# The delta rule of the second block in chunks of 128 tokens instead of 64

## The chip, the cores and the metric

The kernel runs on one core of a Trainium2 chip, as one program that computes two transformer-like blocks after one another. The metric is the device time of one execution in microseconds (us). TensorE (PE) multiplies matrices, VectorE (DVE) and ScalarE (ACT) work elementwise, GpSimd (POOL) does a few masks and fills, and SyncE (SP) issues the transfers between HBM and the on-chip memory SBUF. PSUM holds the results of TensorE.

## What is computed

The change touches one part of the second block, the gated delta rule, for 512 tokens and 8 heads of width 128. For each head a state `S` (128x128) goes from chunk to chunk of tokens. Within a chunk, a unit lower triangular matrix must be inverted. Cut to what matters, the reference is:

```python
GDN_CHUNK = 64
g = jnp.cumsum(chunk(g), axis=-1)                     # log decay, summed inside a chunk
decay = where(causal, exp(g_i - g_j), 0)
L = where(strict, (k_beta @ k.T) * decay, 0)          # chunk x chunk
t_inv = inverse(eye + L)
u = t_inv @ v_beta
w = t_inv @ (k_beta * exp(g))
attn_intra = where(causal, (q @ k.T) * decay, 0)
q_dec = q * exp(g);  k_dec = k * exp(g_last - g)

def step(S, inp):                                     # once per chunk
    v_new = u_c - w_c @ S
    o = q_dec @ S + attn_intra @ v_new
    S = S * exp(g_last) + k_dec.T @ v_new
```

The outputs `o` don't depend on the size of the chunk except by rounding: 8 chunks of 64 tokens and 4 chunks of 128 tokens give the same function.

## The kernel before

**Around the change.** Nearly all of TensorE's work is the projection of activations by weights that come from HBM. A helper (`piece`, `mm3`, `blocks`) loads 128x1024 weights into one of five buffers `raw`, splits each into a high part (`hi`, on ScalarE, L266) and a low part (`lo`, on VectorE, L269), and multiplies by three passes: high by high (L281), high by low (L282), low by high (L284), each 128x128 by 128x512, into a PSUM bank `pp`. A piece is 24 such passes. These passes are called projection passes below. The small products of the delta rule are in full fp32: the profile has each of them as two passes (two weight loads and two matmuls), with the matrices in tiles `sc`, `tr` (PSUM), `rp`, `p`, `n` (work tiles in SBUF), `A` and `G` (big areas).

**The delta rule.** It runs in two halves of four heads (`hf` 0 and 1). For each half the tokens stand in four tiles of 128 (`T[t]`). `gdn_kk` builds minus L for each 128-token tile with masks that keep the two 64-token chunks apart (`tri`, `strict`), writes it to HBM and clears the four 32x32 blocks on the diagonal of the copy that stays (`N`). `gdn_blocks` inverts the 32x32 diagonal blocks of all chunks on VectorE, row by row (L249, L1276), and writes the result to HBM (`X_d`). `gdn_solve` (`SO(j)` for head j) loads these blocks as `XN` and, transposed, as `XT`, and adds what couples two neighbouring blocks of 32: one product `q` (L1296), a copy on ScalarE, one product `z` (L1300), one addition on VectorE (L249), then `u` (L1304) and `w` (L1307). Each of these is four matmuls, one per tile of tokens, that is eight passes.

**The steps.** `gdn_steps` goes over the chunks, four heads at a time: `wS` (L1325), `vn` on VectorE, `o` in pairs that add up in one PSUM tile (L1333 with the state, 128 rows deep; L1334 with `vn`, as deep as a chunk, 64 rows), a copy of `o` on ScalarE (L1335), `sp` (L1339, 64 rows deep) and the new state on VectorE (L1345). Between two steps the program offers one block of the gate projections (`fill`, 16 per half). After the chunks, four norms follow.

**What sets the order.** A scheduler that plays the program through when it is built sets the order of the instructions on each engine, by priority in program order and by when operands and buffers are free. On the chip each engine keeps that order, and so does each transfer queue.

`gates2` prepares the decays: sums of `g` in a chunk (by a product with `tri`), the last `g` of each chunk, and their exponentials, each by some 24 small VectorE instructions (`exp_acc`). `egl` is the exponential for the state.

Of the kernel before, what the change touches and what calls it, by code (L numbers as in the profile page):

```python
# [16 lines left out]
MUL, ADD, SUB, MAX, MIN = ALU.mult, ALU.add, ALU.subtract, ALU.max, ALU.min  # L17
# [68 lines left out]
def lay_out(inp):  # L86
    a = {k: np.asarray(v) for k, v in inp.items()}
    f = np.float32
    o = {}
    o["xT"] = a["x"][0].T.reshape(KT, 128, S)  # L90
    o["cc"] = np.stack([a["c"][0], a["c_2"][0]]).reshape(32, 128)
    o["pos"] = a["positions"].astype(np.int32)
    wada = np.concatenate([a["w_ada"], a["w_ada_2"]])

    wt = wada.transpose(0, 2, 1).reshape(3, 48, 128, 2, 1024).transpose(0, 3, 2, 1, 4)
    o["wada"] = wt.reshape(3, 2, 128, 48 * 1024)

    o["wad0"] = wt[0][:, :, :32].reshape(2, 128, 2, KT, 1024).transpose(3, 1, 2, 0, 4).reshape(KT, 128, 4096)
    inv = (10000.0 ** (-np.arange(32, dtype=f) / f(32))).astype(f)
    sign = np.repeat(np.array([-1, 1, -1, 1], f), 32)  # L100
    cols = [colvec(a["norm_g"][l]) for l in range(2)]
    cols += [colvec(a["b_ada"][l]) for l in range(2)] + [colvec(a["b_ada_2"][0])]
    cols += [colvec(a["final_g"]), colvec(a["norm_gain_2"][0])]
    cols += [colvec(a["b_glu"][l]) for l in range(2)]
    cols += [colvec(a["sub_g"][l]) for l in range(2)]
    cols += [a["conv_w_2"][0].reshape(4, 24, 128).transpose(2, 1, 0).reshape(128, 96)]
    cols += [a["gdn_norm_gain_2"][0][:, None]]
    cols += [np.concatenate([a["q_norm_gain_2"][0]] * 2)[:, None], np.concatenate([a["k_norm_gain_2"][0]] * 2)[:, None]]
    cols += [np.concatenate([inv] * 4)[:, None], sign[:, None]]
    o["vec"] = np.concatenate(cols, axis=1)  # L110
    rep = np.concatenate(
        [np.stack([a["lam_q1"], a["lam_k1"], a["lam_q2"], a["lam_k2"]], 1).reshape(-1),
         a["a_log_2"][0], a["dt_bias_2"][0], a["sinks_2"][0]])
    o["rep"] = np.broadcast_to(rep[None], (128, NREP))
    for l in range(2):
        w = a["w_in"][l]
        u, zs, q, k, v, za = np.split(w, 6, axis=1)
        o[f"wuA{l}"] = grp_blocks(u[:, :512], 512)[0]
        o[f"wuB{l}"] = grp_blocks(u[:, 512:], 512)[0]
        o[f"win{l}"] = np.concatenate([fm_blocks(t) for t in (q, k, zs, za)])  # L120
        o[f"wv{l}"] = grp_blocks(v, 512)
        o[f"wglu{l}"] = fm_blocks(a["w_glu"][l])
        wo = np.concatenate([a["w_out"][l][1024:], a["w_out"][l][:1024]])
        o[f"woA{l}"] = grp_blocks(wo[:, :512], 512)[0]
        o[f"wo{l}"] = fm_blocks(wo[:, 512:])


        def pair(t):
            return t.reshape(2, 32, 64).transpose(0, 2, 1).reshape(128, 32)
        ls = np.broadcast_to(a["ssm_log_step"][l][:, None], (64, 64))  # L130
        o[f"ssa{l}"] = np.concatenate([pair(a["ssm_a_re"][l]), pair(a["ssm_a_im"][l]), pair(ls)], axis=1)
        B = [a[n][l].reshape(2, 32, 64, 16).transpose(0, 2, 1, 3).reshape(128, 512) for n in ("ssm_b_re", "ssm_b_im")]
        C = [a[n][l].reshape(2, 32, 16, 64).transpose(0, 3, 1, 2).reshape(128, 512) for n in ("ssm_c_re", "ssm_c_im")]
        o[f"ssb{l}"] = np.concatenate(B + C, axis=1)
        o[f"ssd{l}"] = a["ssm_d"][l].T
    w2 = a["w_in_2"][0]
    sz = (1024, 1024, 1024, 1024, 8, 8, 1024, 256, 256, 1024, D, D)
    qa, ka, va, za, ba, aa, qb, kb, vb, zb, gla, glb = np.split(w2, np.cumsum(sz)[:-1], axis=1)
    o["w2t"] = grp_blocks(np.concatenate([vb, ba, aa], axis=1), 272)[0]
    o["w2"] = np.concatenate([fm_blocks(t) for t in (qa, ka, va, za, qb, kb, zb, gla, glb)])  # L140
    o["wbg"] = fm_blocks(a["w_branch_gdn_2"][0])
    o["wbs"] = fm_blocks(a["w_branch_swa_2"][0])
    o["wo2A"] = grp_blocks(a["w_out_2"][0][:, :512], 512)[0]
    o["wo2"] = fm_blocks(a["w_out_2"][0][:, 512:])
    o["relb"] = a["rel_bias_2"]
    o["onehot"] = onehot_t5()
    i, j = np.arange(128)[:, None], np.arange(128)[None]
    same = i // 64 == j // 64
    tri = (same & (i <= j)).astype(f)
    strict = (same & (j < i)).astype(f)  # L150
    sellast = (same & (i % 64 == 63)).astype(f)
    o["cst2"] = np.concatenate([tri, strict, sellast, same.astype(f)], axis=1)
    ident = np.eye(128, dtype=f)
    mask = np.zeros((128, 512), f)
    mask[:, 384:] = np.where(np.tril(np.ones((128, 128), bool)), 0.0, -1e30)
    o["cst"] = np.concatenate([ident, mask], axis=1)
    return {k: np.ascontiguousarray(v) for k, v in o.items()}
# [10 lines left out]
class Kern:  # L168
# [949 lines left out]
    def gates2(self):  # L1118
# [49 lines left out]

        ps = self.sbank("sc", 2)
        nc.tensor.matmul(ps[:, :32], self.sellast, gc, start=True, stop=True)  # L1170
        for hf in range(2):
            c = 64 * hf + 63
            nc.tensor.matmul(ps[:, 32 + 32 * hf:64 + 32 * hf], self.ident[:, c:c + 1].to_broadcast([128, 128]), gc, start=True, stop=True)
        self.bg, self.kd, self.egl = sm("bg"), sm("kd"), self.misc[:, 512:576]
        assert len(used) <= 16
        self.exp_acc(gc, sm, self.bg)
        self.tt(self.bg, self.bg, self.beta, MUL)
        self.tt(x, ps[:, :32], gc, SUB)
        self.exp_acc(x, sm, self.kd)
        nc.vector.tensor_copy(e, ps[:, 32:64])  # L1180
        self.exp_acc(e, sm, self.egl[:, 0:32])
        nc.vector.tensor_copy(e, ps[:, 64:96])
        self.exp_acc(e, sm, self.egl[:, 32:64])

    def gdn_k(self, hf, j, ps):

# [94 lines left out]
    def gdn_solve(self, hf, j):  # L1281
# [13 lines left out]
        for t in range(4):  # L1295
            nc.tensor.matmul(q[:, T[t]], N[:, T[t]], XT[:, T[t]], start=True, stop=True)  # L1296
        nc.scalar.copy(N, q)
        z = self.sbank("sc", 2)
        for t in range(4):
            nc.tensor.matmul(z[:, T[t]], XN[:, T[t]], N[:, T[t]], start=True, stop=True)  # L1300
        self.tt(XT, z, XT, ADD)
        u = self.sbank("sc", 2)
        for t in range(4):
# [7 lines left out]
    def gdn_steps(self, hf):  # L1311

        nc, G, A = self.nc, self.G, self.A
        H = [slice(j * 128, (j + 1) * 128) for j in range(4)]
        St = self.t2("n", 4)
        for c in range(8):
            t, R = c // 2, slice(64 * (c % 2), 64 * (c % 2) + 64)
            ct, cc = slice(t * 128, (t + 1) * 128), slice(c * 64, (c + 1) * 64)
            vn = self.t2("p", 4)
            u4 = G[R, 8:12, ct]  # L1320
            vn4 = vn[R].rearrange("p (j e) -> p j e", j=4)
            if c:
                wS = self.sbank("sc", 2)
                for j in range(4):
                    nc.tensor.matmul(wS[R, H[j]], G[:, j, cc], St[:, H[j]], start=True, stop=True)  # L1325
                self.stt(vn4, wS[R].rearrange("p (j e) -> p j e", j=4), -1.0, u4, MUL, ADD)
            else:
                nc.vector.tensor_copy(vn4, u4)
            o = self.sbank("tr", 2)
            for j in range(4):  # L1330
                oj = o[:, j * 64:(j + 1) * 64]
                if c:
                    nc.tensor.matmul(oj, St[:, H[j]], G[:, 4 + j, cc], start=True, stop=False)  # L1333
                nc.tensor.matmul(oj, vn[R, H[j]], G[R, 12 + j, cc], start=c == 0, stop=True)  # L1334
            nc.scalar.copy(A[:, 4 * hf:4 * hf + 4, cc], o[:, :256].rearrange("p (j c) -> p j c", j=4))  # L1335
            if c < 7:
                sp = self.sbank("tr", 2)
                for j in range(4):
                    nc.tensor.matmul(sp[:, H[j]], A[R, 12 + j, ct], vn[R, H[j]], start=True, stop=True)  # L1339
                if c == 0:  # L1340
                    nc.vector.tensor_copy(St, sp)
                else:
                    for j in range(4):
                        g = (c % 2) * 32 + t * 8 + 4 * hf + j
                        self.stt(St[:, H[j]], St[:, H[j]], self.egl[:, g:g + 1], sp[:, H[j]], MUL, ADD)  # L1345
            yield
        for j in range(4):
            oj = A[:, 4 * hf + j, :]
            r = self.rows_norm(oj, self.ones, 1.0 / 128, 1e-6, False)
            self.stt(oj, oj, self.v("gdn_g"), r, MUL, MUL)  # L1350
            yield
# [89 lines left out]
    def block2(self, acc, xs):  # L1441
# [30 lines left out]
        for hf in range(2):  # L1472
# [34 lines left out]
            SO(3)  # L1507
            fill(1)
            st = self.gdn_steps(hf)
            for j in range(12):  # L1510
                next(st, None)
                fill()
            fill(16)
# [184 lines left out]
```

## Time and profile before

| | |
|---|---|
| median of 3 runs | 3592.48 us (3590.34 to 3594.72) |
| the profiled execution | 3601.23 us, its span 3599.2 us |
| TensorE busy | 3432.1 us, 95% of the span |
| VectorE, ScalarE, GpSimd busy | 2128.8, 1185.8, 633.5 us |
| mean granted TensorE clock | 0.976 of full speed |

The span runs from the first to the last instruction of the profiled execution, and the time of that execution is 2.0 us more. A busy TensorE is not one at its peak: matmuls are pipelined, and a matmul of 128 columns and one of 64 can both be listed with some 0.28 us although the next starts much earlier. So what a product costs is read from the starts of its neighbours. The granted clock of a stretch is 1.00 at 2.4 GHz and 0.50 at 1.2 GHz; a mean between the two says how much of the stretch ran at which level.

### The profile page before, as it was taken

How to read it: one execution, taken by the hardware profiler on the slowest of the kernel's cores; microseconds unless marked ns; L12 is line 12 of the kernel's file. 1: busy time of each engine (PE TensorE's matmuls, PEld its weight loads, DVE VectorE, ACT ScalarE, POOL GpSimd, SP SyncE). 2: the span in 40 equal slices, each digit the busy share in tenths (PEclk: the TensorE clock that was granted, in tenths of full speed). 3: DMA queues.
4: the chain of work that ended last, by engine and by line, in shares of the span. 5: the costliest groups of instructions: out<-in, count | busy, mean ns of one | idle time of the engine just before them, and what ended most of it. 6: DMA issues, size and time to landing. Idle time of an engine off the chain costs nothing.

```text
span 3599.2 us, 45635 instructions
## 1 busy us (share of the span) xinstructions
PE 3432.1 (95%) x16673; PEld 2728.0 (76%) x16673; DVE 2128.8 (59%) x4157; ACT 1185.8 (33%) x2052; POOL 633.5 (18%) x885
## 2 busy tenths in 40 slices
PE   7979989999789989899999999999999999999999
PEld 4867766778679876677788887787888777788887
DVE  7994645677857436556665689724892255434432
ACT  3422323353224323333532434222532134433311
POOL 0082681002820006810002212000200000000000
PEclk9989999999899999999999999999999999999999
DMA  9858446656667855356576545322333232224442
GB/s 331 299 153 242 143 120 179 186 190 202 207 206 226 226 163 161 105 176 202 173 225 219 175 123 127 114 89 84 100 108 104 69 100 71 77 92 142 141 140 91
DMA packets 265117, 565.04 MB, mean 157 GB/s; under 512 B 76732, under 2 KB 113853, under 8 KB 264893
## 3 DMA queue, kind: packets, MB, share of 16 engines
q1 hardware_dynamic: 264894, 562.14, 50.7%
q8 instruction: 131, 2.15, 0.2%
q14 instruction: 92, 0.75, 0.1%
HBM read 497.89 MB, written 50.50 MB: 152 GB/s over the span
## 4 chain that ended last, share of the span: by engine, by line
PE 67%; DVE 11%; DMA 9%; POOL 8%; issue 3%; SPq 1%; ACT 1%; DVEq 0%; POOLq 0%; ACTq 0%
PE pp L282 18%; PE pp L281 18%; PE pp L284 18%; DMA raw<-in_wada 5%; DVE lo L269 2%; PE sc L918 1%; POOL misc L820 1%; POOL G L821 1%; POOL misc L818 1%; DVE G L249 1%; POOL misc L819 1%; DVE raw L517 1%; POOL lo L269 1%; POOL G L660 1%; PE sc L1407 1%
## 5 line engine op out<-in xcount | busy, mean ns | idle before, releaser
L281 PE MATMUL pp<-HH,hi 128*128 128x512 f32 (+1 forms) x3568 | 1395.6, 394 | 32.2 <-ACT HH L567 19.1
L282 PE MATMUL pp<-HL,hi 128*128 128x512 f32 (+1 forms) x3440 | 1339.6, 393 | 4.2 <-DVE HL L252 4.1
L266 ACT CAST hi<-raw 128x1024 fp32r<-128x1024 f32 (+1 forms) x538 | 559.7, 1043 | 1194.5 <-PE pp L282 937.5
L284 PE MATMUL pp<-HH,lo 128*128 128x512 f32 (+1 forms) x3568 | 907.8, 392 | 8.6 <-DVE lo L269 8.6
L269 DVE TENSOR_TENSOR lo<-raw,hi 128x1024 fp32r<-128x1024 f32 (+1 forms) x506 | 625.6, 1238 | 349.2 <-PE pp L284 163.9
L281 PEld LDWEIGHTS pp<-HH,hi 128*128 128x128 f32 x3568 | 678.7, 190 | 190.2 <-issue 33.2
L284 PEld LDWEIGHTS pp<-HH,lo 128*128 128x128 f32 x3568 | 659.9, 190 | 162.6 <-issue 19.8
L282 PEld LDWEIGHTS pp<-HL,hi 128*128 128x128 f32 x3440 | 654.2, 190 | 155.4 <-issue 22.1
L517 DVE CUSTOM_DVE_ANT_0 raw<-raw,cs,vec 128x1024 f32<-128x1024 f32 x112 | 158.3, 1414 | 244.0 <-DMA raw<-in_wada 238.3
L517 DVE CUSTOM_DVE_ANT_0 raw<-raw,cs,mod 128x1024 f32<-128x1024 f32 x112 | 154.6, 1381 | 248.6 <-DMA raw<-in_wada 245.3
L217 ACT ACTIVATE p<-p,st 128x128 f32<-128x128 f32 (+2 forms) x192 | 101.9, 531 | 196.9 <-DVE st L244 196.6
L1652 POOL TENSOR_TENSOR rp<-rp,n 128x512 f32<-128x512 f32 (+1 forms) x43 | 59.8, 1404 | 433.8 <-ACT n L1651 433.8
L354 PE MATMUL pp<-lo,HH 128*128 128x512 f32 (+1 forms) x320 | 121.6, 385 | 4.8 <-DVE lo L269 4.7
L353 PE MATMUL pp<-hi,HH 128*128 128x512 f32 (+1 forms) x320 | 121.1, 384 | 4.1 <-ACT HH L567 3.1
L269 POOL TENSOR_TENSOR lo<-raw,hi 128x1024 fp32r<-128x1024 f32 x32 | 77.0, 2406 | 262.8 <-PE pp L284 189.7
L355 PE MATMUL pp<-hi,HL 128*128 128x512 f32 (+1 forms) x320 | 116.3, 384 | 1.0 <-DVE HL L252 0.9
L818 POOL TENSOR_TENSOR misc<-misc,G 128x64 f32<-128x64 f32 x124 | 59.4, 479 | 313.9 <-ACT G L808 304.7
L918 PE MATMUL sc<-rp,rp 64*128 64x128 f32 (+3 forms) x256 | 92.6, 493 | 10.4 <-DVE st L920 10.4
L282 PE MATMUL pp<-A,hi 128*128 128x512 f32 x256 | 100.7, 393 | 0.0
L920 DVE CUSTOM_DVE_ANT_0 p<-sc,cst 128x128 f32<-128x128 f32 (+3 forms) x128 | 61.2, 484 | 33.7 <-PE sc L918 33.3
L354 PEld LDWEIGHTS pp<-lo,HH 128*128 128x128 f32 x320 | 62.2, 195 | 18.7 <-DVE lo L269 5.7
L353 PEld LDWEIGHTS pp<-hi,HH 128*128 128x128 f32 x320 | 61.9, 194 | 17.7 <-ACT HH L567 3.9
(325 smaller groups left out, 3944.5 us busy)
## 6 DMA issues: line engine op xcount, KB each, us to landing
raw<-in_wada SPq DMA_DIRECT2D x224, 512.0 KB, 4.2
raw<-in_w SPq DMA_DIRECT2D x164, 512.0 KB, 3.8
raw<-in_win SPq DMA_DIRECT2D x128, 512.0 KB, 5.0
raw<-in_wo SPq DMA_DIRECT2D x80, 512.0 KB, 4.6
G<-in_wad SPq DMA_DIRECT2D x64, 512.0 KB, 6.0
raw<-in_wv SPq DMA_DIRECT2D x32, 512.0 KB, 3.8
raw<-in_wglu SPq DMA_DIRECT2D x32, 512.0 KB, 4.4
raw<-in_wuA SPq DMA_DIRECT2D x18, 512.0 KB, 4.8
```

What stands on the lines that cost most here:

```text
L217: i = self.nc.scalar.activation(out, src, func, **kw)
L266: nc.scalar.copy(hi[:, :n].bitcast(F32R), raw[:, :n])
L269: eng.tensor_tensor(lo[:, :n].bitcast(F32R), raw[:, :n], hi[:, :n], SUB)
L281: mm(out, hi[:, sl], mh, start=first, stop=False)
L282: mm(out, hi[:, sl], ml, start=False, stop=False)
L284: mm(out, lo[:, sl], mh, start=False, stop=last)
L353: mm(pss[t][:, :n], mh[:, ts], hi[:, sl], start=first, stop=False)
L354: mm(pss[t][:, :n], mh[:, ts], lo[:, sl], start=False, stop=False)
L355: mm(pss[t][:, :n], ml[:, ts], hi[:, sl], start=False, stop=last)
L517: self.nc.vector.tensor_tensor_reduce(w, w, cs, 1.0, self.vec[:, o:o + 1] if first else m, MUL, ADD, m)
L818: T(s1, a8[:, 0], prev, MUL)
L918: nc.tensor.matmul(sc[:, :W], q[rows, i * 128:(i + 1) * 128], k[rows, :W], start=True, stop=True)
```

## The change

A chunk is now a whole 128-token tile. The masks `tri`, `strict` and `sellast` no longer keep two chunks apart. The inverse of a 128-token chunk has four diagonal blocks of 32 instead of two, so the terms that couple them go on to third order: two more products with an addition each stand between `q` and `z` in `gdn_solve`. The steps go over four chunks of 128, with products that are 128 deep and 128 wide, and `egl` needs one exponential instead of two. The loop over steps and norms, with a `fill` each, is 8 long instead of 12; the rest of the 16 fills follows behind it as before.

```diff
-    tri = (same & (i <= j)).astype(f)
-    strict = (same & (j < i)).astype(f)
-    sellast = (same & (i % 64 == 63)).astype(f)
+    tri = (i <= j).astype(f)
+    strict = (j < i).astype(f)
+    sellast = np.broadcast_to(i == 127, (128, 128)).astype(f)
...
         nc.tensor.matmul(ps[:, :32], self.sellast, gc, start=True, stop=True)
-        for hf in range(2):
-            c = 64 * hf + 63
-            nc.tensor.matmul(ps[:, 32 + 32 * hf:64 + 32 * hf], self.ident[:, c:c + 1].to_broadcast([128, 128]), gc, start=True, stop=True)
...
-        nc.vector.tensor_copy(e, ps[:, 32:64])
-        self.exp_acc(e, sm, self.egl[:, 0:32])
-        nc.vector.tensor_copy(e, ps[:, 64:96])
-        self.exp_acc(e, sm, self.egl[:, 32:64])
+        nc.vector.tensor_copy(e, ps[:, :32])
+        self.exp_acc(e, sm, self.egl)
...
         nc.scalar.copy(N, q)
+        src, Y = XN, self.t2("p", 4)
+        for _ in range(2):
+            z = self.sbank("sc", 2)
+            for t in range(4):
+                nc.tensor.matmul(z[:, T[t]], N[:, T[t]], src[:, T[t]], start=True, stop=True)
+            self.tt(Y, z, XN, ADD)
+            src = Y
         z = self.sbank("sc", 2)
         for t in range(4):
-            nc.tensor.matmul(z[:, T[t]], XN[:, T[t]], N[:, T[t]], start=True, stop=True)
+            nc.tensor.matmul(z[:, T[t]], Y[:, T[t]], N[:, T[t]], start=True, stop=True)
         self.tt(XT, z, XT, ADD)
...
-        for c in range(8):
-            t, R = c // 2, slice(64 * (c % 2), 64 * (c % 2) + 64)
-            ct, cc = slice(t * 128, (t + 1) * 128), slice(c * 64, (c + 1) * 64)
+        for t in range(4):
+            ct = slice(t * 128, (t + 1) * 128)
...
-                    nc.tensor.matmul(wS[R, H[j]], G[:, j, cc], St[:, H[j]], start=True, stop=True)
+                    nc.tensor.matmul(wS[:, H[j]], G[:, j, ct], St[:, H[j]], start=True, stop=True)
...
-                if c:
-                    nc.tensor.matmul(oj, St[:, H[j]], G[:, 4 + j, cc], start=True, stop=False)
-                nc.tensor.matmul(oj, vn[R, H[j]], G[R, 12 + j, cc], start=c == 0, stop=True)
+                if t:
+                    nc.tensor.matmul(o[:, H[j]], St[:, H[j]], G[:, 4 + j, ct], start=True, stop=False)
+                nc.tensor.matmul(o[:, H[j]], vn[:, H[j]], G[:, 12 + j, ct], start=t == 0, stop=True)
...
-                    nc.tensor.matmul(sp[:, H[j]], A[R, 12 + j, ct], vn[R, H[j]], start=True, stop=True)
+                    nc.tensor.matmul(sp[:, H[j]], A[:, 12 + j, ct], vn[:, H[j]], start=True, stop=True)
...
             st = self.gdn_steps(hf)
-            for j in range(12):
+            for j in range(8):
                 next(st, None)
                 fill()
             fill(16)
```

The diff moves instructions in two places that matter below. In the order lists, numbers behind a tile's name tell its uses apart, and "x4" are four instructions in a row. The first place is TensorE's row of the solve of the second head of the first half. Before, it reads as follows, with 22 or 23 projection passes at each mark of omission:

```order
L1296 MATMUL sc_18081<-rp_18070,A_86 128x128 x4
...
L1300 MATMUL sc_18087<-A_86,rp_18069 128x128 x4
...
L1304 MATMUL sc_18093<-G_90,rp_18070 128x128 x4
L1307 MATMUL sc_18098<-rp_18070,G_90 128x128 x4
L282 MATMUL pp_18847<-HL,hi_18879 128x512
```

With the change the same solve reads as follows (L1297 are the two new products, L1302 is the old L1300, L1306 and L1309 the old L1304 and L1307; L1196 are transposes for another head):

```order
L1291 MATMUL sc_18067<-rp_18056,A_86 128x128 x4
...
L1297 MATMUL sc_18074<-rp_18055,A_86 128x128 x4
...
L1297 MATMUL sc_18080<-p_18073,A_86 128x128 x4
...
L1196 MATMUL tr_18172<-cst,rp_18165 128x128 x4
...
L1302 MATMUL sc_18086<-A_86,p_18073 128x128 x4
...
L1306 MATMUL sc_18092<-G_90,rp_18056 128x128 x4
L1309 MATMUL sc_18097<-rp_18056,G_90 128x128 x4
```

The two new products have moved in between, and behind each of them stand some 20 to 24 projection passes before the next product of the chain.

The second place is TensorE's row of the second step of the first half. Before, in this order, with 21 projection passes at the first mark and five more rows of the same alternation at the second:

```order
L1325 MATMUL sc_18462<-n_18382,G_90 64x128 x4
L1333 MATMUL tr_18468<-G_90,n_18382 128x64
...
L1334 MATMUL tr_18468<-G_90,p_18461 128x64
L1333 MATMUL tr_18468<-G_90,n_18382 128x64
...
L1339 MATMUL tr_18478<-p_18461,A_86 128x128 x4
```

With the change the same place reads as follows, with 22 projection passes at the first mark:

```order
L1326 MATMUL sc_18487<-n_18407,G_90 128x128 x4
L1333 MATMUL tr_18493<-G_90,n_18407 128x128
...
L1334 MATMUL tr_18493<-G_90,p_18486 128x128
L1333 MATMUL tr_18493<-G_90,n_18407 128x128
...
L1339 MATMUL tr_18503<-p_18486,A_86 128x128 x4
```

The pattern is the same, but every product is now 128 wide, its rows are 128 deep, and a half has four such places instead of eight.

## Rows read from the trace of the kernel before

**Rows 1.** The page: busy time by engine, and the chain that ended last.

```profile
PE 3432.1 (95%) x16673; PEld 2728.0 (76%) x16673; DVE 2128.8 (59%) x4157; ACT 1185.8 (33%) x2052; POOL 633.5 (18%) x885
...
PE 67%; DVE 11%; DMA 9%; POOL 8%; issue 3%; SPq 1%; ACT 1%; DVEq 0%; POOLq 0%; ACTq 0%
```

**Rows 2.** Busy time in stretches: inverse, solves and steps of each half.

```profile
core 0: us, PE busy (x) PEld busy (x) DVE busy (x) ACT busy (x) POOL busy (x), PEclk, DMA share, GB/s
2200.00:2300.00 100.00, 100.00 (x474) 83.35 (x473) 97.44 (x184) 35.67 (x46) 8.65 (x15) 1.00 0.34 102
2300.00:2381.85 81.85, 78.00 (x411) 66.17 (x409) 25.59 (x37) 23.78 (x31) 2.57 (x5) 1.00 0.38 111
2381.85:2495.60 113.75, 113.75 (x538) 90.08 (x538) 31.21 (x55) 19.81 (x27) 0.00 (x0) 0.94 0.25 77
...
2773.70:2887.40 113.70, 113.70 (x538) 90.08 (x537) 28.20 (x45) 19.81 (x26) 0.00 (x0) 0.94 0.23 73
```

**Rows 3.** Groups of TensorE's instructions in the steps of the first half.

```profile
L282 PE MATMUL pp<-HL,hi 128*128 128x512 f32 x101 | 42.1, 417 | 0.0
...
L1334 PE MATMUL tr<-G,p 64*128 64x64 f32 x64 | 13.2, 294 | 0.0
L1333 PE MATMUL tr<-G,n 128*128 128x64 f32 x56 | 12.2, 299 | 0.0
L1325 PE MATMUL sc<-n,G 128*64 128x128 f32 x56 | 8.3, 282 | 0.0
L1339 PE MATMUL tr<-p,A 64*128 64x128 f32 x56 | 8.2, 288 | 0.0
```

**Rows 4.** Timeline of TensorE in the second solve: start, duration, line, operation.

```profile
2334.50 0.40 PE L282 MATMUL pp<-HL,hi 128*128 128x512 f32 x1
...
2339.49 1.05 PE L1304 MATMUL sc<-G,rp 128*128 128x128 f32 x8
2340.38 1.06 PE L1307 MATMUL sc<-rp,G 128*128 128x128 f32 x8
2341.20 0.48 PE L282 MATMUL pp<-HL,hi 128*128 128x512 f32 x1
2341.51 0.40 PE L281 MATMUL pp<-HH,hi 128*128 128x512 f32 x1
```

**Rows 5.** Timeline of TensorE in the second step of the first half.

```profile
2395.29 0.39 PE L282 MATMUL pp<-HL,hi 128*128 128x512 f32 x1
2395.60 0.43 PE L1334 MATMUL tr<-G,p 64*128 64x64 f32 x2
2395.97 0.43 PE L1333 MATMUL tr<-G,n 128*128 128x64 f32 x2
2396.33 0.43 PE L1334 MATMUL tr<-G,p 64*128 64x64 f32 x2
...
2398.06 1.11 PE L1339 MATMUL tr<-p,A 64*128 64x128 f32 x8
2399.09 0.50 PE L281 MATMUL pp<-HH,hi 128*128 128x512 f32 x1
```

**Rows 6.** Stretches of 10 us inside the steps, columns as in rows 2.

```profile
2400.00:2410.00 10.00, 10.00 (x42) 7.81 (x42) 2.23 (x4) 1.64 (x2) 0.00 (x0) 0.85 0.26 80
2410.00:2420.00 10.00, 10.00 (x51) 8.11 (x50) 2.35 (x5) 2.07 (x3) 0.00 (x0) 1.00 0.17 52
2850.00:2860.00 10.00, 10.00 (x38) 7.91 (x37) 1.20 (x5) 1.42 (x2) 0.00 (x0) 0.68 0.14 52
```

**Rows 7.** Timeline of the product L1300 of the first solve and VectorE behind it.

```profile
2315.91 1.05 PE L1300 MATMUL sc<-A,rp 128*128 128x128 f32 x8
...
2317.06 0.69 DVE L249 TENSOR_TENSOR rp<-sc,rp 128x512 f32<-128x512 f32 x1 [4.47 <-PE sc L1300]
2317.76 1.23 DVE L269 TENSOR_TENSOR lo<-raw,hi 128x1024 fp32r<-128x1024 f32 x1
```

**Rows 8.** TensorE's waits, 2300 to 2400 us, then 2692 to 2890 us.

```profile
PE tr L1201 <- DVE G L244: 3.1, 1, 3.1
PE sc L1296 <- DMA rp<-X_d: 0.7, 1, 0.7
...
PE tr L1201 <- DVE G L244: 1.7, 1, 1.7
PE sc L1296 <- DMA rp<-X_d: 1.6, 1, 1.6
```

**Rows 9.** Waits of the transfer queue on SP, 2290 to 2400 us: total, times, longest.

```profile
SPq L265 <- DVE lo L269: 46.4, 14, 7.2
...
SPq L1293 <- POOL rp L1288: 8.3, 3, 4.5
```

**Rows 10.** Timeline of VectorE: small instructions of `gates2` on 128x32.

```profile
2142.82 0.19 DVE L1182 COPY misc<-sc 128x32 f32<-128x32 f32 x1
2142.92 0.18 DVE L393 TENSOR_SCALAR misc<-misc 128x32 int32<-128x32 int32 x1
...
2160.72 1.25 DVE L244 TENSOR_SCALAR misc<-misc 128x32 f32<-128x32 f32 x1
```

More of the change, by code (lines that the diff above doesn't have):

```diff
@@ L1170, in gates2 @@
         nc.tensor.matmul(ps[:, :32], self.sellast, gc, start=True, stop=True)
-        for hf in range(2):
-            c = 64 * hf + 63
-            nc.tensor.matmul(ps[:, 32 + 32 * hf:64 + 32 * hf], self.ident[:, c:c + 1].to_broadcast([128, 128]), gc, start=True, stop=True)
-        self.bg, self.kd, self.egl = sm("bg"), sm("kd"), self.misc[:, 512:576]
+        self.bg, self.kd, self.egl = sm("bg"), sm("kd"), self.misc[:, 512:544]
         assert len(used) <= 16
@@ L1315, in gdn_steps @@
         St = self.t2("n", 4)
-        for c in range(8):
-            t, R = c // 2, slice(64 * (c % 2), 64 * (c % 2) + 64)
-            ct, cc = slice(t * 128, (t + 1) * 128), slice(c * 64, (c + 1) * 64)
+        for t in range(4):
+            ct = slice(t * 128, (t + 1) * 128)
             vn = self.t2("p", 4)
-            u4 = G[R, 8:12, ct]
-            vn4 = vn[R].rearrange("p (j e) -> p j e", j=4)
-            if c:
+            vn4 = vn.rearrange("p (j e) -> p j e", j=4)
+            u4 = G[:, 8:12, ct]
+            if t:
                 wS = self.sbank("sc", 2)
                 for j in range(4):
-                    nc.tensor.matmul(wS[R, H[j]], G[:, j, cc], St[:, H[j]], start=True, stop=True)
-                self.stt(vn4, wS[R].rearrange("p (j e) -> p j e", j=4), -1.0, u4, MUL, ADD)
+                    nc.tensor.matmul(wS[:, H[j]], G[:, j, ct], St[:, H[j]], start=True, stop=True)
+                self.stt(vn4, wS.rearrange("p (j e) -> p j e", j=4), -1.0, u4, MUL, ADD)
             else:
@@ L1330, in gdn_steps @@
             for j in range(4):
-                oj = o[:, j * 64:(j + 1) * 64]
-                if c:
-                    nc.tensor.matmul(oj, St[:, H[j]], G[:, 4 + j, cc], start=True, stop=False)
-                nc.tensor.matmul(oj, vn[R, H[j]], G[R, 12 + j, cc], start=c == 0, stop=True)
-            nc.scalar.copy(A[:, 4 * hf:4 * hf + 4, cc], o[:, :256].rearrange("p (j c) -> p j c", j=4))
-            if c < 7:
+                if t:
+                    nc.tensor.matmul(o[:, H[j]], St[:, H[j]], G[:, 4 + j, ct], start=True, stop=False)
+                nc.tensor.matmul(o[:, H[j]], vn[:, H[j]], G[:, 12 + j, ct], start=t == 0, stop=True)
+            nc.scalar.copy(A[:, 4 * hf:4 * hf + 4, ct], o.rearrange("p (j c) -> p j c", j=4))
+            if t < 3:
                 sp = self.sbank("tr", 2)
                 for j in range(4):
-                    nc.tensor.matmul(sp[:, H[j]], A[R, 12 + j, ct], vn[R, H[j]], start=True, stop=True)
-                if c == 0:
+                    nc.tensor.matmul(sp[:, H[j]], A[:, 12 + j, ct], vn[:, H[j]], start=True, stop=True)
+                if t == 0:
                     nc.vector.tensor_copy(St, sp)
@@ L1343, in gdn_steps @@
                     for j in range(4):
-                        g = (c % 2) * 32 + t * 8 + 4 * hf + j
+                        g = t * 8 + 4 * hf + j
                         self.stt(St[:, H[j]], St[:, H[j]], self.egl[:, g:g + 1], sp[:, H[j]], MUL, ADD)
```

## The prediction

> **What bounds the kernel now.** I read the page first. TensorE is listed as busy for 95% of the span, and the chain that ended last runs over it for 67% [rows 1]. That is an average over stages, so the next view is the busy time by stretch around the delta rule [rows 2]. While VectorE inverts the 32x32 blocks (2200 to 2300 us) it is busy for 97.44 of 100 us and sets the pace together with a TensorE that is hardly ever free. In the solves (2300 to 2381.85) and the steps (2381.85 to 2495.60) VectorE is busy for about 30% of the time, GpSimd for almost none, the transfers for 25 to 38%. TensorE alone fills these stages, because the projections stand between the small products and there are always some ready. So a small product costs exactly the TensorE time by which it pushes the next projection pass back, and the latency between two products costs nothing as long as projection passes stand there. The reader should see in rows 2 that the steps are the one stage of the four shown whose granted clock is below 1.00.
>
> **The price of a pass, from starts.** Between 2334.50 and 2339.49 us stand 22 projection passes [rows 4]: 4.99 / 22 = 0.227 us each. The two products that follow are 16 passes of full fp32, 128 deep and 128 wide. They push the projections from 2339.49 to 2341.20, and the first projection pass after them takes 0.31 instead of 0.227 us, so together 1.71 + 0.08 = 1.79 us, or 0.112 us for a pass, with the cost of going in and out. This is the same kind of pass that the change adds to the solves and leaves in the steps, so I need no other row for it.
>
> The Trainium skill, page "TensorE: Matmul & The Clock Gate", section "Back-to-back issue gap", has N/2.4 ns and 2.5 ns more between warm matmuls, 56 ns for 128 columns, without a word on fp32 there. By that price the changed kernel's 336 small passes would take 18.8 us instead of 37.6 us, an estimate from that page, and the time would come out 19 us lower than below. The row has twice that price, and the measurement decides.
>
> **What the steps cost today.** The stretch of the first half holds 538 TensorE passes [rows 2], of which 64 + 56 + 56 + 56 = 232 belong to the steps [rows 3]. The other 306 are projection passes, 306 x 0.227 = 69.5 us. The steps therefore cost 113.75 - 69.5 = 44.3 us in the first half, and in the second, with the same 538 passes in 113.70 us, 44.2 us: 88.5 us together, 0.19 us for a pass. Two things make them dearer than 0.112.
>
> The first is the alternation in `o`. A pair of 64-deep passes starts at 2395.60, the pair of 128-deep ones at 2395.97, the next at 2396.33 [rows 5]: 0.36 us for two passes, 0.18 for one, although they have only 64 columns. A run of eight 64-deep passes without alternation (L1339) takes from 2398.06 to 2399.09, no less than eight full ones.
>
> The second is the clock. In some stretches of 10 us within the steps it is 0.85 or 0.68 while their neighbours are at 1.00 [rows 6], and over both stages it is 0.94 [rows 2]. The lost time is (1 - 0.94) x 113.75 = 6.8 us in a half, 13.6 us in both. It is contained in the 88.5.
>
> **What the change puts there.** A half now has 3 `wS`, 3 + 4 groups in `o` and 3 `sp`, 13 groups of four matmuls, that is 104 passes, all 128 deep and 128 wide. Their order is as it was, but the partners in `o` have the same depth, so there is nothing left to alternate. 2 x 104 x 0.112 = 23.3 us. The solves get 2 products x 4 matmuls x 2 passes x 8 heads = 128 passes more: 14.3 us. The sum for TensorE is 88.5 - 23.3 - 14.3 = 50.9 us less.
>
> This takes it that the clock stays at 1.00 in the new steps. What speaks for it: the 16 full passes in a row in the solves, the densest fp32 run of the kind that remains, stand in a stage with 1.00 [rows 2, 4], and what I see before the falls is the slow alternation. What speaks against it: a new step has 14 + 8 = 22 such passes in a row, longer than any in the solves. I keep both ends: 0 or 13.6 us.
>
> **What lies beside.** The two new links of a solve are each a product, an addition on VectorE (0.69 us) and the wait for it [rows 7]; 16 in all. The order puts some 20 to 24 projection passes behind each, about 5 us, and they cover it. Without the cover a link would cost the time from the end of the product's passes (8 x 0.112 = 0.90 us after the start of L1300 at 2315.91) to the end of the addition, 2317.75 - 2316.81 = 0.94 us [rows 7], and up to 1.23 us more behind a `lo` split. VectorE has room: 16 x 0.69 = 11 us more in stages where it works 30% of the time. The steps need half as many `vn`, copies and state updates; nobody waits for them today.
>
> In `gates2` some 25 small VectorE instructions go. They start 0.10 us apart, and now and then one takes 1.25 us [rows 10]; 25 x 0.10 = 2.5 us, or about 5 us with two such. They lie in the time in which VectorE sets the pace, but TensorE loses little there, so I take 0 and keep 5 us as a possible gain.
>
> At the end of each inverse TensorE waits today for transposes and for `X_d`: 3.1 + 0.7 and 1.7 + 1.6 us, together 7.1 us [rows 8]. In the new order the first products of the solve stand ahead of the waiting transposes. The wait may go or double; I take no change, and 7 us to both sides.
>
> **The sum.** The profiled execution took 3601.23 us, 8.7 us above the median of the runs; 3601.2 - 50.9 = 3550.3 us is what I expect of a profiled execution like it. Against the median, 3592.5 - 50.9 = 3541.6, so 3542 us.
>
> **Rivals.**
>
> *The clock falls as often as before.* The new steps are still fp32 in long rows. Then 10 to 14 us of the gain stay away: 3552 to 3556 us. For it speaks that the falls come in several of today's steps and in neither solve stage nor inverse [rows 2, 6], so it is the kind of work that brings them, and a new step is still long rows of fp32; against it the solves at 1.00. The Trainium skill, "TensorE: Matmul & The Clock Gate", section "What's actually happening", says that the clock follows how busy the array has recently been; no run here yet shows how it rates a full fp32 pass.
>
> *The new links are not covered.* If the chip arrives at them later than the scheduler thought, each costs up to 0.94 + 1.23 = 2.2 us, all 16 some 35 us: 3577 us, and half of them 3559 us. Against it: TensorE waits for no product of the solves today except the first [rows 8].
>
> *Slower: weights stuck behind the blocks of the inverse.* The loads of `X_d` for the third head need a buffer `rp` that the first solve holds until its `w`. They stand in SP's queue, and the raw weights stand behind them. Today they wait up to 4.5 us [rows 9]. A solve grows by two products and some 46 projection passes, 2 x 0.9 + 46 x 0.227 = 12.2 us, so a stall of 16.7 us is possible for the third and fourth head of each half. Four such, fully felt, are 67 us: 3592.5 - 50.9 + 67 = 3609 us. It decides from 12.7 us felt per stall. Against it: SP mostly waits for a weight buffer to come free (46.4 us in 14 waits [rows 9]), so it runs ahead, and each of the five buffers holds 24 passes, 5.4 us; a stall must outlast several.
>
> *More than the sum.* `gates2` and the end of the inverse give 5 to 12 us on top: 3530 to 3537 us.
>
> **How the numbers follow.** The forecast (clock holds, cover holds, 3536 to 3549) has 60%, the clock rival 20%, uncovered links 8%, the stuck weights 4%, more than the sum 8%. The likeliest is 3542 us. The range goes from 3531, below which only the far end of the last case lies, to 3561, which holds the clock rival with some lost waits and half of the uncovered links. 0.2% of the time, about 7 us, is what a measurement can tell from no change. All cases but the stuck weights end below it; of that one, half lies above, a part within. With 2% for causes not thought of: faster 0.94, same 0.03, slower 0.03.
>
> **What would show it.** The order has 131 projection passes from the first to the last product of a half's steps, so these take 131 x 0.227 + 11.6 = 41 us instead of 113.7. There are four `o` instead of eight, the starts of their passes are 0.11 us apart rather than 0.18, and the granted clock is 1.00 there. Each solve has two more groups of eight passes and about 12 us more from `q` to `w`, without a wait of TensorE in front of L1297 or L1302. The rest of the trace is the same, only earlier. The prediction is wrong if the clock in the steps stays at 0.94, if TensorE waits for the additions, or if raw weights come late in the solves.

## The result, and the profile after

The changed kernel takes 3540.65 us (median of 4 runs, 3539.55 to 3542.55) against 3591.41 us before (4 runs, 3583.02 to 3594.72). The ratio is 0.9864, with a 95% interval of 0.9849 to 0.9879: 51 us faster.

The busy time by stretch of the changed kernel's trace answers to [rows 2]: first the solves and the steps of the first half, then those of the second. The last columns are the granted clock, the share of the transfers and GB/s.

```profile
core 0: us, PE busy (x) PEld busy (x) DVE busy (x) ACT busy (x) POOL busy (x), PEclk, DMA share, GB/s
2297.40:2420.20 122.80, 122.78 (x634) 105.25 (x635) 38.20 (x47) 33.36 (x42) 2.63 (x5) 0.99 0.35 110
2420.20:2461.90 41.70, 41.70 (x237) 36.40 (x236) 13.98 (x27) 9.13 (x12) 0.00 (x0) 1.00 0.27 89
...
2661.00:2784.70 123.70, 123.25 (x636) 105.39 (x637) 38.22 (x47) 33.36 (x42) 2.63 (x5) 0.99 0.34 110
2784.70:2826.50 41.80, 41.80 (x238) 36.45 (x237) 12.37 (x18) 9.22 (x13) 0.00 (x0) 1.00 0.27 89
```

The steps of a half take 41.7 us instead of 113.75, and their clock is at 1.00 instead of 0.94. The solves take 122.8 instead of 72 us (2309.9 to 2381.9). Both lengths contain projections, so they are no gain or loss yet. TensorE's groups in the steps of the first half (2420.2 to 2461.9 us) answer to [rows 3]:

```profile
L282 PE MATMUL pp<-HL,hi 128*128 128x512 f32 x44 | 17.3, 394 | 0.0
L281 PE MATMUL pp<-HH,hi 128*128 128x512 f32 x44 | 17.3, 394 | 0.0
L284 PE MATMUL pp<-HH,lo 128*128 128x512 f32 x45 | 12.0, 397 | 0.0
L1334 PE MATMUL tr<-G,p 128*128 128x128 f32 x32 | 5.7, 274 | 0.0
L1333 PE MATMUL tr<-G,n 128*128 128x128 f32 x24 | 4.6, 275 | 0.0
L1339 PE MATMUL tr<-p,A 128*128 128x128 f32 x24 | 3.2, 275 | 0.0
L1326 PE MATMUL sc<-n,G 128*128 128x128 f32 x24 | 3.2, 274 | 0.0
```

There are 133 projection passes and 104 small ones. By the price of the prediction 133 x 0.227 = 30.2 us, so 41.7 - 30.2 = 11.5 us are left for the steps; 11.6 were forecast, and 44.3 was the cost before. The timeline of TensorE in the second step shows why (compare [rows 5]):

```profile
2433.13 0.39 PE L284 MATMUL pp<-HH,lo 128*128 128x512 f32 x1
2433.36 0.38 PE L1334 MATMUL tr<-G,p 128*128 128x128 f32 x2
2433.58 0.39 PE L1333 MATMUL tr<-G,n 128*128 128x128 f32 x2
2433.80 0.39 PE L1334 MATMUL tr<-G,p 128*128 128x128 f32 x2
...
2434.92 1.06 PE L1339 MATMUL tr<-p,A 128*128 128x128 f32 x8
2435.73 1.87 PE L284 MATMUL pp<-HH,lo 128*128 128x512 f32 x7
```

The pairs in `o` follow each other after 0.22 us, where they took 0.36, although each pass now does twice the columns and the `vn` ones twice the depth. The list of TensorE's waits from 2120 to 3000 us, total, times and longest, has these for the part around the change:

```profile
PE sc L1291 <- DMA rp<-X_d: 8.1, 2, 4.3
...
PE tr L1105 <- ACT n L1095: 0.9, 1, 0.9
```

There is none for the additions in the solves. The wait at the end of the inverse is still there, 8.1 us instead of 7.1 [rows 8], now all of it for `X_d`, once in each half.

The spans of the two profiled executions differ by 60.4 us, more than the medians. 9.2 us of that are there before the first product of `gates2` (2130.9 against 2121.7 us after the start), in the first block, which the change doesn't touch.

Behind the last step of the second half the two traces differ as well. These are the 42.6 us there, first before, then after:

```profile
2887.40:2930.00 42.60, 39.67 (x152) 30.22 (x153) 23.28 (x30) 17.75 (x26) 0.00 (x0) 0.92 0.26 84
2826.50:2869.10 42.60, 42.60 (x180) 33.54 (x179) 22.94 (x28) 18.13 (x27) 0.00 (x0) 1.00 0.28 94
```

Each holds ten passes of the norms, so the changed kernel gets 170 projection passes through in this time and the kernel before only 142. In the kernel before, TensorE waits 2.9 us for a norm there (L1105), and its clock falls.

### The profile page after: what moved, and what is told of

The parts are those of the page before. It is cut to its first block, busy times and chain, and to the rows that moved or that the text cites. A ratio compares the mean times of both kernels' runs of the same rounds, so it can differ in the third digit from the quotient of the medians.

```text
span 3538.8 us, 45321 instructions
## 1 busy us (share of the span) xinstructions
PE 3373.7 (95%) x16541; PEld 2699.5 (76%) x16541; DVE 2121.2 (60%) x4108; ACT 1184.6 (33%) x2044; POOL 631.2 (18%) x885
## 4 chain that ended last, share of the span: by engine, by line
PE 66%; DVE 10%; DMA 10%; POOL 8%; issue 3%; SPq 2%; ACT 1%; DVEq 0%; POOLq 0%; ACTq 0%
PE pp L282 18%; PE pp L281 18%; PE pp L284 18%; DMA raw<-in_wada 6%; DVE lo L269 2%; PE sc L918 2%; DVE G L249 2%; POOL misc L818 1%; POOL G L821 1%; POOL misc L820 1%; POOL misc L819 1%; DVE raw L517 1%; POOL lo L269 1%; POOL G L661 1%; PE pp L353 1%
## 5 line engine op out<-in xcount | busy, mean ns | idle before, releaser
L281 PE MATMUL pp<-HH,hi 128*128 128x512 f32 (+1 forms) x3568 | 1390.5, 393 | 29.5 <-ACT HH L567 18.4
L1101 POOL TENSOR_TENSOR wt<-n,wt 128x512 fp32r<-128x512 f32 x16 | 24.7, 1545 | 321.4 <-ACT wt L1100 168.7
L354 PEld LDWEIGHTS pp<-lo,HH 128*128 128x128 f32 x320 | 62.5, 196 | 18.7 <-DVE lo L269 5.8
```

The costliest lines, as they stand in the source:

```text
L281: mm(out, hi[:, sl], mh, start=first, stop=False)
L354: mm(pss[t][:, :n], mh[:, ts], lo[:, sl], start=False, stop=False)
```

## The experiments

Each was compared with the kernel before on its chip; ratios are to that kernel, with 95% intervals. A difference between two changed kernels is that of their ratios, where the text doesn't say that they ran on one chip.

**The long solve alone.** To the kernel before, the two products are added; with chunks of 64 tokens the extra terms are zero.

```diff
         nc.scalar.copy(N, q)
+        src, Y = XN, self.t2("p", 4)
+        for _ in range(2):
+            z = self.sbank("sc", 2)
+            for t in range(4):
+                nc.tensor.matmul(z[:, T[t]], N[:, T[t]], src[:, T[t]], start=True, stop=True)
+            self.tt(Y, z, XN, ADD)
+            src = Y
...
-            nc.tensor.matmul(z[:, T[t]], XN[:, T[t]], N[:, T[t]], start=True, stop=True)
+            nc.tensor.matmul(z[:, T[t]], Y[:, T[t]], N[:, T[t]], start=True, stop=True)
```

> The kernel before, with the two extra products and additions of the changed solve; chunks stay at 64 tokens, for which the extra terms are zero. My sum: 128 passes x 0.112 = 14.3 us slower than before (ratio 1.0040), with no wait of TensorE for the additions. Rival, links uncovered: up to 2.2 us more for each of 16 links, 14.3 + 35 = 49 us slower (1.0137). Rival, the extra passes fall into idle time: no change.

Measured: 1.0136 (1.0115 to 1.0156), 49 us slower, to the microsecond what the rival of uncovered links said. But the trace has no wait at those links. Its stretches show something else: the steps of the first half, the norms behind them, and the last steps and norms of the second half.

```profile
2418.60:2530.00 111.40, 110.63 (x524) 87.47 (x523) 32.62 (x58) 17.66 (x25) 0.00 (x0) 0.94 0.21 68
2530.00:2544.50 14.50, 8.74 (x21) 5.76 (x22) 14.50 (x41) 2.35 (x5) 0.00 (x0) 0.55 0.29 82
...
2922.00:2968.00 46.00, 31.41 (x104) 19.80 (x104) 20.84 (x35) 12.80 (x22) 0.00 (x0) 0.63 0.04 11
```

Its waits from 2500 to 2970 us begin with the norms:

```profile
PE tr L1105 <- ACT n L1095: 13.3, 6, 2.8
PE pp L281 <- DVE p L252: 5.4, 1, 5.4
```

In these 46 us at the end of the second half TensorE has 104 passes, the transfers stand at 0.04, and the clock is at 0.63. From 2922.6 to 2961.1 us not one projection pass runs. The solves of the first half took 431 of them for cover instead of 251. These are TensorE's groups between the same products, first in the kernel before (2309.85 to 2381.85 us), then with the long solve (2296.4 to 2418.6 us):

```profile
L281 PE MATMUL pp<-HH,hi 128*128 128x512 f32 x85 | 33.4, 393 | 0.0
L282 PE MATMUL pp<-HL,hi 128*128 128x512 f32 x85 | 33.4, 393 | 0.0
L284 PE MATMUL pp<-HH,lo 128*128 128x512 f32 x81 | 21.4, 396 | 0.0
...
L282 PE MATMUL pp<-HL,hi 128*128 128x512 f32 x144 | 57.5, 400 | 0.0
L281 PE MATMUL pp<-HH,hi 128*128 128x512 f32 x144 | 57.4, 398 | 0.0
L284 PE MATMUL pp<-HH,lo 128*128 128x512 f32 x143 | 37.3, 397 | 0.0
```

The order, fixed when the program is built, puts some 23 projection passes behind each new link. By the prediction's own 0.94 to 2.2 us for a link, 4 to 10 would do. Less its projections at 0.227 us, the trace has the solves of both halves 18.6 us dearer than before; another 27 us come later: 10 between the first half's last step and the second half's solves, 5 in the second half's steps, 12 behind them. (The traced execution is 7 us faster than the median.) So the greater part of the 49 us isn't paid where the links are: the last steps and norms stand bare, much of the time at half the clock. I took this as a new theory: **the cover is a stock that the long solve uses up**.

**The short steps alone.** The changed kernel without the lines shown above, with `XN` in place of `Y`; the terms of second and third order are left out of the inverse.

> The changed kernel without the two extra products: the terms of second and third order in the inverse of a chunk are left out. My sum: 88.5 - 23.3 = 65.2 us faster than before, that is 14.3 us faster than the changed kernel (ratio to before 0.982). If the new links had cost waits, it would be more than 20 us faster than the changed kernel; if they were free, the two would be equal.

Measured: 0.9809 (0.9791 to 0.9828), about 20 us below the changed kernel. By the two intervals it is 11 to 28 us, so the links aren't free, but the time alone doesn't tell 14 us from more than 20. The traces say more: the solves hold 251 and 252 projection passes again, and less these at 0.227 us they take 29.5 us in both halves, against 48.7 in the changed kernel. So the long solve costs some 19 us there, not 14.3, although nothing waits at its new links.

**Eight chunks without alternation.** In the kernel before, `vn` gets zeros in its other half, and the product with it is 128 deep like its partner.

```diff
             vn = self.t2("p", 4)
+            nc.gpsimd.memset(vn, 0.0)
...
-                nc.tensor.matmul(oj, vn[R, H[j]], G[R, 12 + j, cc], start=c == 0, stop=True)
+                nc.tensor.matmul(oj, vn[:, H[j]], G[:, 12 + j, cc], start=c == 0, stop=True)
```

> The kernel before with 8 chunks of 64 and one thing taken away: the products of o with vn are made 128 deep by zeros in the other half of vn (filled by GpSimd), so that no pass of 64 rows alternates with one of 128. The number of passes is the same. Theory that alternation costs time and brings the clock down: 14 steps x 14 passes x (0.18 - 0.112) = 13 us, and the 13.6 us of the clock as well, so about 27 us faster than before (ratio 0.9925), granted clock 1.00 in the steps. Rival, the clock falls for fp32 passes as such or for the 64-deep sp: 13 us faster (0.9963) and the clock stays at 0.94. Rival, 0.18 us is the price of 64 columns whatever the depth: no change.

Measured: 0.9918 (0.9903 to 0.9933), 29 us faster, as the first theory said. In its trace the steps of the first half are one stretch at 1.00:

```profile
2382.00:2482.90 100.90, 100.90 (x538) 83.22 (x536) 29.70 (x54) 19.81 (x26) 2.10 (x4) 1.00 0.27 87
```

The same 538 passes as in [rows 2] take 100.9 us instead of 113.75. Its timeline has the pairs 0.22 us apart with 64 columns, the same as with 128 in the changed kernel:

```profile
2395.89 0.39 PE L1334 MATMUL tr<-G,n 128*128 128x64 f32 x2
2396.11 0.39 PE L1335 MATMUL tr<-G,p 128*128 128x64 f32 x2
2396.33 0.39 PE L1334 MATMUL tr<-G,n 128*128 128x64 f32 x2
```

The `sp` 64 rows deep and the `wS` 64 columns wide are still there, so they alone don't bring the clock down. So more than half of the gain of the change can be had without longer chunks, by making the depths in `o` agree: one zero fill in each step gives it.

**Alternation put back.** The changed kernel with `o` taking only the first 64 tokens of `vn`, as its expectation says.

```diff
-                nc.tensor.matmul(o[:, H[j]], vn[:, H[j]], G[:, 12 + j, ct], start=t == 0, stop=True)
+                nc.tensor.matmul(o[:, H[j]], vn[:64, H[j]], G[:64, 12 + j, ct], start=t == 0, stop=True)
```

> The changed kernel, with the alternation put back: the product of o with vn uses only the first 64 tokens of a chunk, so the other 64 are left out of it. The number of passes is the same. Theory that alternation costs time: 6 steps x 14 passes x (0.18 - 0.112) = 6 us slower than the changed kernel, and if alternation brings the clock down, some falls of 1.7 us each in the steps as well, 6 to 14 us in all. Rival, alternation is not the cause: equal to the changed kernel.

Measured: 0.9890 (0.9872 to 0.9908), about 10 us slower than the changed kernel (1 to 18 us by the two intervals). Its timeline and the stretch of its first steps:

```profile
2448.34 0.49 PE L1334 MATMUL tr<-G,p 64*128 64x128 f32 x2
2448.75 0.49 PE L1333 MATMUL tr<-G,n 128*128 128x128 f32 x2
2449.17 0.48 PE L1334 MATMUL tr<-G,p 64*128 64x128 f32 x2
```

```profile
2434.80:2481.00 46.20, 46.20 (x236) 37.56 (x235) 14.92 (x28) 9.03 (x12) 0.00 (x0) 1.00 0.26 80
```

The pairs are 0.42 us apart, and a half's steps take 46.2 instead of 41.7 us for one pass less; the second half has 46.3 instead of 41.8. The clock stays at 1.00 in both, however. Alternation costs time by itself; it brought the clock down only in the form that it has in the kernel before, with 64 columns and 60 pairs in a half. Here it is 28 pairs, but in 46.2 us instead of 113.75, so they don't come less often.

**Two halves of the cover theory.** In two kernels 3 of the 16 gate projections of each half are left out (288 passes, 65 us of TensorE work): the changed kernel, and the kernel before with the long solve.

```diff
                     for j in gl:
-                        self.blocks([w2[base + j]], hacts, lambda _, ps: ev(j, ps))
+                        if j < 13:
+                            self.blocks([w2[base + j]], hacts, lambda _, ps: ev(j, ps))
+                        else:
+                            t = self.t2("s2", 1)
+                            nc.gpsimd.memset(t, 0.0)
+                            nc.sync.dma_start(sig_d[which, j], t)
                         break
```

> The changed kernel with 3 of the 16 gate projections of each half left out (their results are zeros). This takes away 6 x 48 = 288 projection passes, 65 us of TensorE work, and with it cover for the chains of the solves and steps. Theory that the changed kernel has cover to spare: 65 us faster than the changed kernel (3475 us, ratio to before 0.968). If its cover were as short as that of the kernel with the long solve and 64-token chunks, clearly less.

> The kernel before with the long solve, and 3 of the 16 gate projections of each half left out in the same way. Theory that the long solve used up the projections that should stand between the last steps and the norms: much of the 65 us comes back as waiting there, so it is only 20 to 45 us faster than the kernel with the long solve (which stood at 1.0136 of before), ratio to before 1.001 to 1.008. Rival, the 30 us that the long solve cost beyond its passes have nothing to do with cover: the full 65 us faster, ratio 0.9955.

Measured: 0.9755 (0.9735 to 0.9774) for the changed kernel, 39 us faster than with all projections and not 65; and 1.0012 (1.0002 to 1.0023) for the long solve with short chunks, 45 us faster than the long solve with all of them, at the upper end of the 20 to 45 us that the theory gave, and clear of the rival's 0.9955. For the second kernel the theory holds: the trace has two stretches in its last steps and norms at half the clock, with few transfers.

```profile
2482.00:2523.00 41.00, 32.92 (x110) 24.95 (x110) 20.09 (x57) 3.90 (x8) 0.00 (x0) 0.50 0.10 27
2851.00:2929.00 78.00, 59.74 (x185) 42.17 (x185) 23.47 (x46) 12.08 (x23) 0.00 (x0) 0.50 0.01 4
```

For the first my expectation fell: the changed kernel has some cover to spare, but less than three blocks per half. With three fewer, the last steps and the norms of the second half stand bare. These bare steps, which have equal depths, still run at full clock (first line); the norms behind them don't (second line).

```profile
2799.80:2810.60 10.80, 8.27 (x65) 7.31 (x63) 3.63 (x10) 2.30 (x5) 0.00 (x0) 1.00 0.15 50
2806.00:2834.50 28.50, 15.10 (x42) 7.49 (x42) 16.29 (x27) 10.75 (x19) 0.00 (x0) 0.64 0.00 0
```

**Where the solve starts.** The changed kernel with the solves one place later.

```diff
             Vb(1)
-            SO(0)
             Vb(2)
-            SO(1)
+            SO(0)
             Vb(3)
-            SO(2)
+            SO(1)
             fill(1)
-            SO(3)
+            SO(2)
             fill(1)
+            SO(3)
```

> The changed kernel with each solve called one place later in the program (the first behind the third V projection instead of the second), so that projections and transposes stand between the end of the inverse and the first product of the solve. Theory that the wait for X_d (8.1 us in the two halves of the changed kernel) and the two clock falls beside it are a matter of what stands there: up to 8 + 3 = 11 us faster than the changed kernel (3530 us against 3541). Rival, the work is only moved and TensorE waits for something else there, as in the kernel before: equal to the changed kernel.

Measured: 0.9848 (0.9833 to 0.9863), which can't be told from the changed kernel's 0.9864. The rival holds: its waits for `X_d` fall to 1.5 us, and the transposes wait for VectorE instead.

```profile
PE tr L1196 <- DVE G L244: 6.1, 2, 3.4
...
PE sc L1291 <- DMA rp<-X_d: 1.5, 1, 1.5
```

**A shorter chain.** If cover is a stock, a chain with half as many links one after another must need less of it. In the changed kernel two heads are solved side by side, behind all four V projections; the passes are the same.

```diff
-    def gdn_solve(self, hf, j):
+    def gdn_solve(self, hf, js):
...
+        def prod(L, M):
+            z = [self.sbank("sc", 2) for _ in R]
+            for i in R:
+                for t in range(4):
+                    nc.tensor.matmul(z[i][:, T[t]], L[i][:, T[t]], M[i][:, T[t]], start=True, stop=True)
+            return z
+        q = prod(N, XT)
...
+            SO((0, 1))
             fill(1)
...
+            SO((2, 3))
```

> The changed kernel with the solves of two heads side by side: each link is done for both before the next link, and all four V projections stand ahead of the first solve. The same passes, but half as many links one after another, so the chain needs about half the projections as cover, and work stands ahead of the first product. Theory that the changed kernel has cover to spare: no gain from the shorter chain itself, and at most the 8 to 11 us at the end of the inverse; 3530 to 3541 us. Rival, cover still binds somewhere in the changed kernel: more than 11 us faster.

Measured: 0.9838 (0.9825 to 0.9852). Whether that is faster than the changed kernel is settled by running both once more on one chip, beside two further kernels: the paired long solve in the kernel before, and the paired solves with three projections per half fewer.

> The changed kernel as it is, on the same chip and in the same rounds as the three that follow, so that they can be set against it. By its earlier runs its ratio to before is 0.9864.

> The changed kernel with paired solves once more, beside the changed kernel on the same chip. From the sum of waits (8.1 us before the first products of the solves against 1.2, and one clock fall less) 5 to 9 us faster than the changed kernel; if it is the same within 0.2%, the shorter chain is worth nothing as long as the cover lasts.

> The kernel before with the long solve, but two heads side by side as in the paired kernel (same passes, half as many links one after another, all V projections first); chunks stay at 64 tokens. Theory that the long solve in sequence lost some 30 us only by using up the projections that cover the last steps and the norms: now the cover lasts, and only the 128 passes remain, 14 us slower than before (ratio 1.004). Rival, the extra links or passes as such cost what they did: 1.0136.

> The kernel with 128-token chunks and paired solves, with 3 of the 16 gate projections of each half left out (zeros in their place). Theory that the changed kernel without them lost 25 us of the 65 because its sequential solves had used up the cover: with the shorter chain all 65 us come back, ratio to before about 0.9838 - 0.0182 = 0.966. Rival, cover has nothing to do with the length of the chain: 0.973 to 0.975, as for the changed kernel with less cover.

Measured: 0.9858 (0.9845 to 0.9870) for the changed kernel and 0.9855 (0.9842 to 0.9868) for the paired one: the same. A shorter chain is worth nothing while the cover lasts, and no complete version was found that clearly beats the changed kernel. Where the cover doesn't last, it decides. The kernel before with the long solve comes to 1.0025 (1.0016 to 1.0035) instead of 1.0136, that is 9 us for the 128 passes instead of 49; the 14 us forecast lie just above the interval. Its solves of the first half (2305.8 to 2382.9 us) hold 245 projection passes instead of 431, as few as before:

```profile
L281 PE MATMUL pp<-HH,hi 128*128 128x512 f32 x80 | 31.5, 394 | 0.0
L282 PE MATMUL pp<-HL,hi 128*128 128x512 f32 x80 | 31.4, 393 | 0.0
L284 PE MATMUL pp<-HH,lo 128*128 128x512 f32 x85 | 22.4, 395 | 0.0
```

The paired kernel without the six projections comes to 0.9659 (0.9646 to 0.9672), 70 us below the one with them: all the 65 us, where the sequential one gave 39. The traces of all four paired runs have no wait of L1105. The paired kernels also start their solves later, behind all four V projections; a later start alone gave nothing in the changed kernel, and it wasn't tried alone in the kernel before. With that said, the cover theory was right in all three. The 5 to 9 us that the shorter waits let expect of the paired kernel didn't come.

## Why the prediction was right

It was 3542 us, with 3531 to 3561; 3540.65 us was measured. That the two lie 1 us apart is in part luck. The traces, each stage less its projections at 0.227 us, have the steps 65.6 us cheaper (65.2 forecast) and the solves 18.7 us dearer (14.3 forecast). That is 46.9 us, not 50.9. The missing 4 us came from places for which the sum had nothing: 9.2 us less behind the last step of the second half, and 4.8 us more before the solves of the two halves. A second trace of the changed kernel has the same stages within 1.2 us each. Point by point:

- **The price of a pass.** 0.112 us for a full fp32 pass held, 11.5 us for 104 passes in the first half, and alike in the second. The 56 ns that follow from the Trainium skill ("TensorE: Matmul & The Clock Gate", section "Back-to-back issue gap"), by which the time would have been 19 us lower, don't hold for full fp32 in this trace. That section gives them for isolated matmuls; for a stream of weight loads and matmuls it has about 81 ns at 128 columns, and the 112 ns here are more than that too.
- **The cost of the steps before**, 88.5 us, fits: 22.9 us are left of it and 65.6 are gone. The two things that made it dear are shown by the kernel with equal depths: 12.85 us less in the stage of the first half, 6.8 of which are the clock by [rows 2], which leaves 6.0 for the alternation. The prediction gave the alternation no term of its own; its sum took both at once.
- **The solves.** 434 x 0.227 = 98.5 us of the 122.8 are projections, so 24.3 us remain, against 72.0 - 251 x 0.227 = 15.0 before. The second half has 24.4. The growth of 9.3 us per half contains four more passes of transposes, and a first product and the projections next to it at half the clock, beside 64 x 0.112 = 7.2 us. The term of 14.3 us for both halves was small by 4.4 us.
- **The clock.** The likeliest case came: 1.00 in the steps, no falls. The rival of falls as before was wrong, although 22 full fp32 passes now stand in a row.
- **The end of the inverse.** 8.1 instead of 7.1 us of waiting, close to no change; the slow clock right behind it is in the solves above.
- **The cover.** The prediction said that projections cover the new links, and in the changed kernel they do. But it took the cover as free and never asked whose it was. The long solve takes 183 projection passes more in the first half (434 instead of 251), and the steps give back 173 (133 instead of 306), so solves and steps together take 567 instead of 557. Without that return the same links cost 49 us. The norms behind the second half's steps even stand better than before (142 against 170 passes in 42.6 us, above), a gain that the prediction had at nothing. That the rival "links not covered" gave 49 us for the long solve alone was a coincidence: nothing waited at the links, and most of the cost arose in the norms and last steps.
- **Weights behind the blocks of the inverse** didn't come: SP's longest wait for `rp` is 4.9 us, against 4.5 before.

What stays open: why the clock falls with the alternation of 64 columns and not with that of 128, and what `gates2` gives by itself. From its first product to the first of the solves the profiled executions have 175.7 instead of 179.0 us, but 29 projection passes fewer stand there (6.6 us), and what TensorE waits for has changed as well. So these 3.3 us are no gain of `gates2`, and no run took that part alone.

## What to carry to other kernels

Work that fills the waits of a chain is a stock: count how much a longer chain takes, and look where it is missing later, which may be 100 us away and in code that nobody touched. Solving two independent heads side by side took the long solve back from 431 projection passes to 245, and is the first thing to try when cover runs short. And before making a tile bigger, look whether neighbouring products on TensorE differ in depth: to make them equal, even with zeros, gave more than half of the gain here.

## What the runs showed of the hardware

- A full-fp32 pass with 64 columns and one with 128 take the same 0.11 us, if 128-deep passes stand beside 128-deep ones. 64-deep ones in turn with 128-deep ones cost 0.18 us each with 64 columns and 0.21 us with 128.
- TensorE can be listed as busy for all of a stretch and yet be granted 1.2 GHz in parts of it: in the steps before, with the alternation of short passes, the clock fell again and again (0.94 as the mean of the stage in [rows 2]); equal depths, at the same number of passes, kept it at 2.4 GHz.
- Bare steps with alternating depths and the bare norms behind them ran wholly at half the clock (0.50 for 78 us in the long solve with less cover), so there a missing cover cost twice: for the latency, and for the slower passes. Bare steps with equal depths kept the full clock for the 10.8 us that the trace of the changed kernel with less cover has of them.
